# q of two mLSTM heads as plain blocks ahead of the seven-product doubles, and the blocks beside the attention moved on

## The chip, the cores and the metric

The kernel runs on one core of a Trainium2 chip. The time is device microseconds of one launch, as the median of several runs. Five engines work side by side, each through its own queue of instructions in order: TensorE (PE, matmuls, with its weight loads as PEld), VectorE (DVE), ScalarE (ACT), GpSimd (POOL) and SyncE (SP). Here SP issues the loads of weights and POOL most of the stores.

## The reference

Two layers over 1024 latent tokens and 256 context tokens of width 1024. Layer 0 runs 16 neighbourhood-attention heads beside 4 mLSTM heads of 256 columns; layer 1 is a gated recurrence (HGRN2). The change is in layer 0 alone, in how the input projection of the mLSTM heads is computed and when.

```python
def _ab_mixer(h_lat, h_ctx, w_in, b_gate, q_norm, k_norm, rpb, h_norm, w_out, need_ctx):
    def project(h, rotary):
        qa, ka, va, za, qb, kb, vb, ob, zb, g = _split_cols(h @ w_in, AB_SIZES)
...
        qb, kb = _heads(qb, ML_HEADS), _heads(kb, ML_HEADS) * (ML_DIM ** -0.5)
        if rotary:
            qb, kb = _axial_rope(qb), _axial_rope(kb)
...
    oa_l = _neighbourhood_attention(qa_l, ka_l, va_l, ka_c, va_c, rpb)
    hb_l, hb_c = _mlstm_bidir(mb_l, mb_c, need_ctx)
...
        ya = oa.reshape(oa.shape[:2] + (NA_WIDTH,)) * jax.nn.silu(za)
        yb = hb.reshape(hb.shape[:2] + (ML_WIDTH,)) * jax.nn.silu(zb)
        return jnp.concatenate([ya, yb], axis=-1) @ w_out
```

So each mLSTM head needs five blocks of 256 columns of `h @ w_in`: q and k (rotated for the latent tokens only), v, o and z. All is in fp32.

## The kernel before

**Precision.** Every fp32 operand is split into a high and a low part (`split`, L74 the high part on ACT, L75 the low part on DVE), and every product is three matmuls: high by high, high by low, low by high (`dense`, L127 to L129). The normed input lies transposed in memory as `hh` and `hl`, 1280 columns of tokens (ten row tiles of 128) by eight slices of 128 along the width.

**Plain blocks.** `proj_out` computes one block of 256 columns: for each pair of row tiles 2 x 8 x 3 matmuls into the psum buffer `mm`, one eviction into the buffer `ev` (there are two) with or without a gate (copy for v, tanh for o, tanh and a product for z), and one store by POOL to `md`, where the mLSTM reads it later. `ml_ahead(part, h)` is such a block of head h; `na_values(b)` ("n2") is the same for values of the attention.

**Doubles.** q and k of two heads together are 512 columns, and they are computed by Strassen's scheme in Winograd's form with seven products of half size instead of eight (`q_two` makes the first two products and `q_seven` the other five). The sums of quarters of the input that it needs are made on DVE and ACT by `q_sums`: "2" builds s2, s4 and s3 in memory of their own, "1" overwrites quarter 21 of `hh`/`hl` in place, which is restored by a DMA when all doubles are done. Each product's psum is added up on DVE (`sa`, `tr` and `mm` are the psum buffers, `qu` and `qv` the partial sums), the last addition writes `ev`, and for q and k the four instructions of `rope` (L999 to L1002) rotate `ev` in place ahead of the store.

**Stages of layer 0 on the chip,** in us of the span: norm and gates to about 220; the stage of `a_ahead` (sums, two plain blocks, four doubles: q and k of heads 0 and 1, q and k of heads 2 and 3) to 488; the attention in eight groups of two heads (`na_attn(p2, ...)`, ten tiles each) to 1372; the mLSTM (`ml_all`, steps g) to about 1765, with the output projection beside its second half.

**What sets the order.** A scheduler with a model of times orders the instructions of each stage; program order is the priority. The table `ahead` says which plain block is issued in which attention group, as work for PE beside the softmax; `issue_after(self.at[i])` holds a block back until tile i of the last group. `ML_AHEAD` does the same for the mLSTM: key -1 is its start, key g its step g, under `filler()`, which gives the block the lowest priority. The weights of the output projection are loaded into the buffers "w" that plain blocks use and into memory that `hh` leaves.

Of the kernel before, what the change touches and what calls it, by code (L numbers as in the profile page):

```python
# [9 lines left out]
F32 = mybir.dt.float32  # L10
# [8 lines left out]
P = 128  # L19
D = 1024  # L20
KD = D // P
LAT = 1024
# [3 lines left out]
EPS = 1e-6  # L26
NEG = -1.0e30

ML_AHEAD = {-1: ("o", 3), 2: ("z", 3)}
ML_ORDER = [8, 9, 4, 5, 6, 7, 0, 1, 2, 3]  # L30
ML_OUT = {1: (8, 8, 9, 9, 10, 10, 11, 11, 12, 12), 0: (13, 14, 14, 15, 16, 17, 18, 20, 22, 24)}

# [14 lines left out]
class Prog:  # L47
# [221 lines left out]
    def proj_out(self, c0, dst, gate=None, rev=False):  # L269
        nc = self.nc  # L270
        w = self.wring([self.a["wab"][:, c0 : c0 + 256]], 256)
        for tt in range(0, NT, 2)[:: -1 if rev else 1]:

            ps = self.ps("mm", [P, 2, 256])
            for j in range(2):
                self.proj_nat(ps[:, j, :], w, tt + j, 0, 256)
            v = self.t(self.wp, [P, 2, 256], F32, "ev", self.evb)
            if gate is None:
                nc.scalar.copy(v, ps)
            else:  # L280
                gate(v, ps)
            nc.gpsimd.dma_start(out=dst[tt * P : (tt + 2) * P, :].rearrange("(j p) f -> p j f", p=P), in_=v)


# [3 lines left out]
    def gate_z(self, out, ps):  # L288
        self.gate_o(out, ps)
        self.nc.vector.scalar_tensor_tensor(out=out, in0=out, scalar=1.0, in1=ps, op0=ALU.add, op1=ALU.mult)  # L290


    @contextmanager
# [6 lines left out]

    def ml_ahead(self, part, h, rev=False):
        c0 = (4 + "qkvoz".index(part)) * D + h * 256
        gate = {"o": self.gate_o, "z": self.gate_z}.get(part)
        dst = self.md[(part, h)] = self.md_all[len(self.md)]
        self.proj_out(c0, dst, gate, rev)

# [672 lines left out]
    def ml_sink(self, part, h, pool):  # L979
        dst = []  # L980
        for c in range(2):
            dst.append(self.md_all[len(self.md)])
            self.md[(part, h + c)] = dst[c]

        def sink(c, t, m, o):
            if part in "qk" and t < LAT // P:
                self.rope(o, t, m, pool)
            self.q_store(dst[c], t, m, o)

        return sink  # L990

    def rope(self, o, t, m, pool):
        tt = self.nc.vector.tensor_tensor
        s = self.t(self.qsr[0], [P, 512], F32, *self.qsr[1:])[:, 0 : m * 256]
        v4 = lambda x: x.rearrange("p (x b c) -> p x b c", b=2, c=64)
        tab = lambda i: (
            self.ropet[:, i, t : t + m].rearrange("p t a c -> p (t a) c").unsqueeze(2).to_broadcast([P, 2 * m, 2, 64])
        )
        tt(out=v4(s), in0=v4(o), in1=tab(1), op=ALU.mult)  # L999
        tt(out=v4(o), in0=v4(o), in1=tab(0), op=ALU.mult)  # L1000
        tt(out=v4(o)[:, :, 0, :], in0=v4(o)[:, :, 0, :], in1=v4(s)[:, :, 1, :], op=ALU.subtract)
        tt(out=v4(o)[:, :, 1, :], in0=v4(o)[:, :, 1, :], in1=v4(s)[:, :, 0, :], op=ALU.add)  # L1002

    def a_ahead(self, pool):
        nc, a = self.nc, self.a
        self.ropet = self.t(pool, [P, 2, 8, 2, 64], F32, "mrope", 1)
        nc.sync.dma_start(out=self.ropet, in_=a["rope"])
        a21 = self.q_quarter("21")
        for c in range(2):
            for i in range(self.half):  # L1010
                s = slice(i * P, (i + 1) * P)
                nc.gpsimd.dma_start(out=self.a21[c, :, :, s], in_=a21[c][:, :, s])
        S = {}
        self.q_sums(pool, "2", S)
        self.ml_ahead("v", 1, True)
        self.ml_ahead("o", 0, True)
        S["1"] = a21
        self.q_sums(pool, "1", S)
        todo = [(p, h) for h in (0, 2) for p in "qk"]
        cols = [[(4 + "qkvoz".index(p)) * D + (h + c) * 256 for c in range(2)] for p, h in todo]  # L1020
        sinks = [self.ml_sink(p, h, pool) for p, h in todo]
        us = [self.q_two(self.q_raw(pool, cols[i], ("11", "21")), S, sinks[i], pool) for i in range(2)] + [None] * 2
        for i in range(len(todo)):
            self.q_seven(self.q_raw(pool, cols[i]), S, sinks[i], pool, us[i])
        for c in range(2):
            nc.gpsimd.dma_start(out=a21[c], in_=self.a21[c])
# [191 lines left out]
    def build(self):  # L1218
        self.six = None
        tc, nc, a = self.tc, self.nc, self.a  # L1220
        dma = nc.sync.dma_start
        with ExitStack() as es:
# [21 lines left out]
            def load(name, shape, eng=nc.gpsimd):  # L1244
# [13 lines left out]
                out=self.qkn, in0=qkn[:, 0:1], scalar1=qkn[:, 1:2], scalar2=0.125, op0=ALU.mult, op1=ALU.mult  # L1258
# [57 lines left out]
            with tc.tile_pool(name="na", bufs=2) as pool, tc.tile_pool(name="wx", bufs=2) as wx, self.pp.phase(tq=1, s=2, acc=1):  # L1316
                self.six = [(self.wp, "w", 4)] * 4 + [(wx, "w", 2)] * 2
                qk = self.na_qk(0, pool)
                z = self.na_z(0, pool)
                self.ml_ahead("z", 0)  # L1320
                ahead = {1: ["n2"], 2: ["n3"], 3: ["o1"], 4: ["z1"], 5: ["v2"], 6: ["o2"], 7: ["z2", "v3"]}
                for p2 in range(8):
                    self.na_attn(p2, qk, z, pool)
                    if p2 < 7:
                        qk = self.na_qk(p2 + 1, pool)
                    for i, x in enumerate(ahead.get(p2, [])):
                        with tc.issue_after(self.at[(3, 6)[i]]) if p2 == 7 else nullcontext():
                            self.na_values(int(x[1])) if x[0] == "n" else self.ml_ahead(x[0], int(x[1]))
                    if p2 < 7:
                        z = self.na_z(p2 + 1, pool)  # L1330
# [268 lines left out]
```

## Time and profile before

| what | value |
|---|---|
| timed runs | 3545.17, 3551.78, 3552.8 us, median 3551.78 |
| profiled execution | 3541.76 us, its span 3539.9 us |
| instructions | 64788, of them 24378 matmuls |
| PE, PEld busy | 98%, 89% |
| DVE, ACT, POOL busy | 68%, 45%, 15% |
| mean DMA rate | 102 GB/s |

A window's row gives, for a stretch of the span, each engine's busy time and in brackets its instructions, then the clock granted to PE as a share of full speed, the busy share of the DMA engines and what they moved. A row of the waits says which engine and line waited for which, for how long in total, how often, and the longest. A row of the timeline is one instruction or a run of like ones, with the idle time ahead of it in square brackets. A row of a tile's view gives the count and the shortest, median and longest duration in ns, with the first and last start. All matmuls are pipelined, so the time one takes from the next is read from the count in a full window, not from its duration.

### The profile page before, as it was taken

To read this page: it belongs to the slowest core of one execution; us is meant where nothing else is said; L and a number is where in the kernel's file an instruction comes from. 1 tells how busy PE (TensorE), PEld (TensorE's weight loads), DVE (VectorE), ACT (ScalarE), POOL (GpSimd) and SP (SyncE) were. 2 spreads that over 40 slices of the span, in tenths; PEclk is the share of its full clock that TensorE was granted. 3 is DMA by queue.
4 is the path that set the end of the run, shared out by engine and by line. 5 is a ranking of instruction groups with operands and counts; after the bars stand their busy time and mean duration, and the time that the engine had idled before them with its cause. 6 is when DMAs were issued, how large, how long until landed. Compare 5 with 4: busy or idle time off the path is not lost.

```text
span 3539.9 us, 64788 instructions
## 1 busy us (share of the span) xinstructions
PE 3460.8 (98%) x24378; PEld 3144.3 (89%) x24378; DVE 2390.2 (68%) x6044; ACT 1597.8 (45%) x3691; POOL 524.6 (15%) x838
## 2 busy tenths in 40 slices
PE   8998999999999999999999999999999999999989
PEld 5898999999999989887778999989999999999877
DVE  4668866766666654666767766577777777777853
ACT  5532225555455534555547333344444444444431
POOL 3210121222222211111211111000000100000010
PEclk9999999999999999999999999999999999999999
DMA  7542332222223224544474222212111211211354
GB/s 234 179 155 78 93 115 72 74 77 79 83 80 86 72 83 154 162 139 147 125 250 147 102 100 101 87 31 60 61 48 52 63 49 49 60 60 49 108 176 125
DMA packets 372649, 359.71 MB, mean 102 GB/s; under 512 B 30072, under 2 KB 322872, under 8 KB 372208
## 3 DMA queue, kind: packets, MB, share of 16 engines
q1 hardware_dynamic: 328944, 248.25, 23.8%
q0 software_dynamic: 43392, 107.32, 9.0%
q8 instruction: 193, 3.16, 0.4%
q14 instruction: 120, 0.98, 0.1%
HBM read 274.00 MB, written 81.32 MB: 100 GB/s over the span
## 4 chain that ended last, share of the span: by engine, by line
PE 81%; issue 9%; DMA 3%; DVE 2%; ACT 2%; POOL 1%; SPq 0%; POOLq 0%; ACTq 0%; DVEq 0%
PE mm L129 14%; PE mm L127 14%; PE mm L128 14%; PE s L1126 6%; PE acc L689 2%; PE tr L669 2%; PE sa L128 2%; PE sa L127 2%; PE sa L129 2%; PE acc L472 2%; PE s L479 1%; PE s L1171 1%; PE mm L743 1%; PE mm L744 1%; PE mm L745 1%
## 5 line engine op out<-in xcount | busy, mean ns | idle before, releaser
L127 PE MATMUL mm<-wh,hh 128*128 128x256 f32 x2120 | 608.1, 287 | 2.4 <-ACT ev L545 1.5
L128 PE MATMUL mm<-wl,hh 128*128 128x256 f32 x2120 | 608.4, 287 | 0.7 <-DVE wl L75 0.7
L129 PE MATMUL mm<-wh,hl 128*128 128x256 f32 x2120 | 608.4, 287 | 0.4 <-DVE hl L75 0.4
L129 PE MATMUL mm<-hh,wl 128*128 128x512 f32 (+1 forms) x1344 | 490.9, 365 | 0.0
L127 PE MATMUL mm<-hh,wh 128*128 128x512 f32 (+1 forms) x1344 | 485.0, 361 | 0.0
L128 PE MATMUL mm<-hl,wh 128*128 128x512 f32 (+1 forms) x1344 | 483.9, 360 | 0.0
L127 PEld LDWEIGHTS mm<-wh,hh 128*128 128x128 f32 x2120 | 404.6, 191 | 9.9 <-issue 3.7
L128 PEld LDWEIGHTS mm<-wl,hh 128*128 128x128 f32 x2120 | 404.8, 191 | 5.1 <-DVE wl L75 0.9
L129 PEld LDWEIGHTS mm<-wh,hl 128*128 128x128 f32 x2120 | 404.4, 191 | 5.3 <-issue 1.5
L74 ACT CAST wh<-wraw 128x512 fp32r<-128x512 f32 x282 | 173.5, 620 | 261.2 <-PE mm L128 127.2
L128 PEld LDWEIGHTS mm<-hl,wh 128*128 128x128 f32 x1344 | 254.0, 189 | 32.2
L129 PEld LDWEIGHTS mm<-hh,wl 128*128 128x128 f32 x1344 | 253.9, 189 | 30.2
L127 PEld LDWEIGHTS mm<-hh,wh 128*128 128x128 f32 x1344 | 254.3, 189 | 29.2
L1117 ACT COPY gksel<-gK 128x512 f32<-128x512 f32 x224 | 147.0, 663 | 214.3 <-PE s L1126 205.2
L75 DVE TENSOR_TENSOR wl<-wraw,wh 128x512 fp32r<-128x512 f32 x282 | 190.6, 686 | 60.0 <-ACT wh L74 58.3
L1126 PE MATMUL s<-gQ,gksel 128*128 128x128 f32 x1536 | 199.8, 276 | 0.0
L1126 PEld LDWEIGHTS s<-gQ,gksel 128*128 128x128 f32 x1536 | 192.4, 191 | 7.0
L743 PE MATMUL mm<-woh,yh 128*128 128x512 f32 x444 | 180.2, 407 | 6.1 <-ACT woh L74 3.3
L745 PE MATMUL mm<-woh,yl 128*128 128x512 f32 x444 | 177.9, 401 | 1.0 <-DVE yl L75 0.9
L744 PE MATMUL mm<-wol,yh 128*128 128x512 f32 x444 | 177.7, 400 | 0.0
L74 ACT CAST wh<-b 128x512 fp32r<-128x512 f32 x130 | 80.8, 622 | 199.5 <-PE sa L129 100.3
L1147 DVE TENSOR_TENSOR gQ<-gQ,gT 128x256 f32<-128x256 f32 x384 | 143.3, 414 | 28.1 <-PE s L1126 28.1
(457 smaller groups left out, 8646.9 us busy)
## 6 DMA issues: line engine op xcount, KB each, us to landing
wraw<-yd SPq DMA_DIRECT2D x144, 256.0 KB
wraw<-in_wc_dram SPq DMA_DIRECT2D x128, 256.0 KB
wraw<-in_wab_dram SPq DMA_DIRECT2D x92, 256.0 KB
md<-ev POOLq DMA_DIRECT2D x92, 256.0 KB, 2.8
adar<-in_wada_dram POOLq DMA_DIRECT2D x32, 512.0 KB, 4.8
b<-in_wc_dram SPq DMA_DIRECT2D x64, 256.0 KB
vzd<-qo POOLq DMA_DIRECT2D x56, 256.0 KB, 2.5
adar<-in_wada_dram SPq DMA_DIRECT2D x16, 512.0 KB
```

What stands on the lines that cost most here:

```text
L74: nc.scalar.copy(hi, x)
L75: nc.vector.tensor_tensor(out=lo, in0=x, in1=hi.bitcast(F32), op=ALU.subtract)
L127: mm(ps, lhsT=lh(k), rhs=rh(k), start=(first and k == 0), stop=False)
L128: mm(ps, lhsT=lh(k), rhs=rl(k), start=False, stop=False)
L129: mm(ps, lhsT=ll(k), rhs=rh(k), start=False, stop=(last and k == nk - 1))
L472: nc.tensor.matmul(num, lhsT=qc[:, j, :], rhs=C[d][:, j, :], start=False, stop=(j == 1))
L743: mm(ps, lhsT=yh[:, k, :], rhs=w.h(kk), start=(kk == 0), stop=False)
L744: mm(ps, lhsT=yh[:, k, :], rhs=w.l(kk), start=False, stop=False)
L745: mm(ps, lhsT=yl[:, k, :], rhs=w.h(kk), start=False, stop=(kk == 8 * len(qs) - 1))
L1117: nc.scalar.copy(ksel.rearrange("p (b s i) -> p b s i", s=2, i=h), pick(K))
L1126: nc.tensor.matmul(pa[:, c, :].rearrange("p (b s i) -> p b s i", s=2, i=h), lhsT=ksel[:, c * P : (c + 1) * P], rhs=qp[:, c * nbc : (c + 1) ...
L1147: nc.vector.tensor_tensor(out=t[:, i, :, s, :], in0=t[:, i, :, s, :], in1=bc(tot), op=ALU.mult)
```

## The change

In `a_ahead` one of the four doubles goes (q of heads 2 and 3); those two q are computed as plain blocks with a new gate, `gate_q`, which copies on ACT and rotates in place on DVE, with the scratch buffer `qv2` in place of `qs`. They stand between v of head 1 and the sums "1", where o of head 0 stood. o of head 0 becomes the first block beside the attention; the blocks that follow move on by one place, and v of head 3 moves into the start of the mLSTM, whose o and z follow at steps 1 and 4 instead of the start and step 2. In the last attention group the two blocks are held back to tiles 0 and 5 instead of 3 and 6. `rope` takes the scratch buffer as an argument.

```diff
-ML_AHEAD = {-1: ("o", 3), 2: ("z", 3)}
+ML_AHEAD = {-1: ("v", 3), 1: ("o", 3), 4: ("z", 3)}
...
-                gate(v, ps)
+                gate(v, ps, *[tt] * (gate == self.gate_q))
...
+    def gate_q(self, out, ps, tt):
+        self.nc.scalar.copy(out, ps)
+        if tt < LAT // P:
+            self.rope(out.rearrange("p a b -> p (a b)"), tt, 2, self.qrt)
...
-        gate = {"o": self.gate_o, "z": self.gate_z}.get(part)
+        gate = {"o": self.gate_o, "z": self.gate_z, "q": self.gate_q}.get(part)
...
-    def rope(self, o, t, m, pool):
+    def rope(self, o, t, m, home):
         tt = self.nc.vector.tensor_tensor
-        s = self.t(self.qsr[0], [P, 512], F32, *self.qsr[1:])[:, 0 : m * 256]
+        s = self.t(home[0], [P, 512], F32, *home[1:])[:, 0 : m * 256]
...
+        self.qrt = (pool, "qv2", 2)
...
         self.q_sums(pool, "2", S)
         self.ml_ahead("v", 1, True)
-        self.ml_ahead("o", 0, True)
+        self.ml_ahead("q", 2, True)
+        self.ml_ahead("q", 3, True)
         S["1"] = a21
         self.q_sums(pool, "1", S)
-        todo = [(p, h) for h in (0, 2) for p in "qk"]
+        todo = [("q", 0), ("k", 0), ("k", 2)]
...
-        us = [self.q_two(self.q_raw(pool, cols[i], ("11", "21")), S, sinks[i], pool) for i in range(2)] + [None] * 2
+        us = [self.q_two(self.q_raw(pool, cols[i], ("11", "21")), S, sinks[i], pool) for i in range(2)] + [None]
...
-                self.ml_ahead("z", 0)
-                ahead = {1: ["n2"], 2: ["n3"], 3: ["o1"], 4: ["z1"], 5: ["v2"], 6: ["o2"], 7: ["z2", "v3"]}
+                self.ml_ahead("o", 0)
+                ahead = {1: ["z0"], 2: ["n2"], 3: ["n3"], 4: ["o1"], 5: ["z1"], 6: ["o2"], 7: ["z2", "v2"]}
...
-                        with tc.issue_after(self.at[(3, 6)[i]]) if p2 == 7 else nullcontext():
+                        with tc.issue_after(self.at[(0, 5)[i]]) if p2 == 7 else nullcontext():
```

How the order moves, at three places. First DVE among the quarter sums ahead of the products, in the order before (`qs` are the sums, L75 the low parts of a split):

```order
L75 TENSOR_TENSOR s2l_2109<-qs_2127,s2h_2108 128x4x128
L860 TENSOR_TENSOR qs_2127<-qs_2127,hh_126 128x512
L860 TENSOR_TENSOR qs_2127<-qs_2127,hl_127 128x512
L75 TENSOR_TENSOR s4l_2115<-qs_2127,s4h_2114 128x4x128
L838 TENSOR_TENSOR qs_2141<-hl_127 128x512
L839 TENSOR_TENSOR qs_2140<-qs_2140,qs_2141 128x512
```

The same place on DVE after, where L1005 to L1008 are a rotation at the eviction of a plain q (lines 6 further down than before):

```order
L75 TENSOR_TENSOR s2l_2109<-qs_2127,s2h_2108 128x4x128
L866 TENSOR_TENSOR qs_2127<-qs_2127,hh_126 128x512
L866 TENSOR_TENSOR qs_2127<-qs_2127,hl_127 128x512
L1005 TENSOR_TENSOR qv_450_2618<-ev_2616,mrope_2089 128x512
L75 TENSOR_TENSOR s4l_2115<-qs_2127,s4h_2114 128x4x128
L1006 TENSOR_TENSOR ev_2616<-ev_2616,mrope_2089 128x512
L844 TENSOR_TENSOR qs_2141<-hl_127 128x512
L1007 TENSOR_TENSOR ev_2616<-ev_2616,qv_450_2618 128x4x64
L1008 TENSOR_TENSOR ev_2616<-ev_2616,qv_450_2618 128x4x64
L845 TENSOR_TENSOR qs_2140<-qs_2140,qs_2141 128x512
```

The four instructions of a rotation now stand between the sums, one or two sums apart. Second, PE in the first tiles of the last attention group, in the order before (`s` are scores, `tr` transposes, `acc` the product with the values):

```order
L632 MATMUL s_16171<-akh_15372,aqs_15370 128x264
L633 MATMUL s_16171<-akl_15374,aqs_15370 128x264
L619 MATMUL s_16211<-akh_15371,aqs_15369 128x256
L620 MATMUL s_16211<-akl_15373,aqs_15369 128x256
L669 MATMUL tr_16186<-ident_73,aP_16164 96x128 x2
L669 MATMUL tr_16186<-ident_73,aP_16164 72x128
```

The first tile of that group on PE after (`mm` with `hh` and `hl` is a plain block):

```order
L625 MATMUL s_15837<-akh_15070,aqs_15068 128x256
L626 MATMUL s_15837<-akl_15072,aqs_15068 128x256
L638 MATMUL s_15842<-akh_15070,aqs_15068 128x264
L639 MATMUL s_15842<-akl_15072,aqs_15068 128x264
L127 MATMUL mm_16532<-wh_16509,hh_126 128x256
L128 MATMUL mm_16532<-wl_16508,hh_126 128x256
L129 MATMUL mm_16532<-wh_16509,hl_127 128x256
```

Block matmuls now stand in this group from its first tile. Third, PE at the end of the last plain block beside the mLSTM, in the order before (`tr`, `s` and `acc` with names that begin with m are the mLSTM's own):

```order
L128 MATMUL mm_18253<-wl_18035,hh_126 128x256
L129 MATMUL mm_18253<-wh_18036,hl_127 128x256
L526 MATMUL tr_18880<-ident_73,mhs_3241_18641 128x128
L407 MATMUL s_18892<-mqT_3296_18788,mkT_18795 128x128 x2
L526 MATMUL tr_18835<-ident_73,mhs_3252_18666 128x128
L479 MATMUL s_18913<-mvw_18911,mkn_3120_18335 128x258
```

The same end on PE after:

```order
L128 MATMUL mm_18489<-wl_18271,hh_126 128x256
L129 MATMUL mm_18489<-wh_18272,hl_127 128x256
L406 MATMUL tr_19476<-ident_73,mkn_3512_19474 128x128 x2
L485 MATMUL s_19545<-mvw_19541,mkn_3419_19196 128x258
L400 MATMUL tr_19487<-ident_73,mqn_19485 128x128 x2
L406 MATMUL tr_19494<-ident_73,mkn_3519_19492 128x128 x2
```

Before, 37 rows lie between that end and the first matmul of the output projection, in step 8 of the mLSTM; after, 15 rows, in step 10.

More of the change, by code (lines that the diff above doesn't have):

```diff
@@ L986, in sink @@
             if part in "qk" and t < LAT // P:
-                self.rope(o, t, m, pool)
+                self.rope(o, t, m, self.qsr)
             self.q_store(dst[c], t, m, o)
         return sink
-    def rope(self, o, t, m, pool):
+    def rope(self, o, t, m, home):
         tt = self.nc.vector.tensor_tensor
-        s = self.t(self.qsr[0], [P, 512], F32, *self.qsr[1:])[:, 0 : m * 256]
+        s = self.t(home[0], [P, 512], F32, *home[1:])[:, 0 : m * 256]
         v4 = lambda x: x.rearrange("p (x b c) -> p x b c", b=2, c=64)
```

## The prediction

> **What bounds the kernel now.** The page comes first: one engine is full, and the chain that ended last runs on it.
>
> ```profile
> span 3539.9 us, 64788 instructions
> PE 3460.8 (98%) x24378; PEld 3144.3 (89%) x24378; DVE 2390.2 (68%) x6044; ACT 1597.8 (45%) x3691; POOL 524.6 (15%) x838
> PE 81%; issue 9%; DMA 3%; DVE 2%; ACT 2%; POOL 1%; SPq 0%; POOLq 0%; ACTq 0%; DVEq 0%
> ```
>
> TensorE is 98% busy and carries 81% of the chain. A matmul more costs its time unless it falls into a hole, and a hole closed is a gain. So I read the windows next, stage by stage, looking for holes near the places that the change touches.
>
> ```profile
> core 0: us, PE busy (x) PEld busy (x) DVE busy (x) ACT busy (x) POOL busy (x), PEclk, DMA share, GB/s
> 280.00:360.00 80.00, 67.60 (x510) 64.04 (x509) 68.84 (x131) 14.27 (x24) 8.77 (x14) 0.96 0.27 79
> 360.00:440.00 80.00, 80.00 (x674) 80.00 (x674) 67.70 (x139) 16.56 (x28) 14.56 (x22) 1.00 0.30 95
> 1270.00:1290.00 20.00, 15.38 (x120) 12.19 (x119) 13.72 (x56) 9.31 (x31) 3.28 (x5) 0.91 0.44 126
> 1300.00:1320.00 20.00, 20.00 (x185) 19.39 (x184) 10.57 (x38) 7.00 (x22) 4.68 (x7) 1.00 0.29 86
> 1478.00:1504.00 26.00, 20.01 (x92) 15.79 (x92) 21.33 (x64) 18.86 (x52) 5.37 (x12) 0.87 0.90 275
> ```
>
> Row two is the price list. It lies wholly in the products: 674 matmuls of 256 columns in 80 us, 0.1187 us each, TensorE full, VectorE at 67.70/80 = 85%. The other rows show three holes.
>
> *Hole 1, where the products begin (280 to 360):* 510 matmuls where the same product work has 674, so 164 are missing: 164 x 0.1187 = **19.5 us** (idle 12.4 plus 0.04 x 80 of clock gives 15.6; some records may be absent). The waits from 285 to 356, the timeline and a window of 10 us name the cause.
>
> ```profile
> DVE ev L932 <- DMA md<-ev: 7.0, 4, 2.9
> PE sa L127 <- DVE qu L956: 3.5, 1, 3.5
> 331.70 0.58 PE L127 MATMUL sa<-wh,s4h 128*128 128x256 f32 x1 [3.50 <-DVE qu L956]
> 330.00:340.00 10.00, 8.30 (x48) 8.30 (x49) 9.05 (x21) 1.24 (x2) 2.00 (x3) 0.66 0.19 66
> ```
>
> TensorE waits for an accumulator that VectorE has not added up: VectorE, 68.84 of 80 busy, carries the quarter sums, the weight splits and the first rotations at once. The 3.50 us wait is followed by a granted clock of 0.66 over 10 us, so it costs 3.4 us more.
>
> The Trainium skill, "TensorE: Matmul & The Clock Gate", section on the HAM clock gate, says that half clock follows an idle window of about 3.4 us; by that rule only waits of that length cost clock, and this one agrees.
>
> *Hole 2, the last attention group (1270 to 1290):* idle 4.62 and 0.09 x 20 = 1.8 of clock, **6.4 us**. The same windows for tile mm alone:
>
> ```profile
> core 0: us, PE busy (x), PEclk, DMA share, GB/s
> 1270.00:1290.00 20.00, 2.01 (x18) 0.91 0.44 126
> 1300.00:1320.00 20.00, 14.17 (x107) 1.00 0.29 86
> ```
>
> With 107 projection matmuls among the attention TensorE is full; with 18 it is not. The filler is missing there.
>
> *Hole 3, the recurrence of the mLSTM (1478 to 1504):* idle 5.99 and 0.13 x 26 = 3.4 of clock, **9.4 us**. Rows of the timeline, and one of the waits:
>
> ```profile
> 1478.30 0.28 PE L129 MATMUL mm<-wh,hl 128*128 128x256 f32 x1
> ...
> 1487.15 0.33 PE L526 MATMUL tr<-ident,mhs 128*128 128x128 f32 x1 [2.44 <-ACT myt L527]
> 1489.71 0.69 PE L394 MATMUL tr<-ident,mqn 128*128 128x128 f32 x2 [2.23 <-ACT myt L527]
> ...
> 1503.57 0.58 PE L743 MATMUL mm<-wh,yh 128*128 128x512 f32 x1
> ACT woh L74 <- DMA wraw<-in_woab_dram: 3.7, 2, 2.8
> ```
>
> It opens at the last matmul of the last plain block and closes at the first of the output projection. Between them ScalarE stands in its queue behind a cast that waits 3.7 us for the output weights, and the copies that TensorE needs stand behind it.
>
> **The change part by part.** Sums go against the profiled execution, 3541.76 us (its span and 1.86 around it). The median of the runs is 3551.78, 10.0 above it; I take the difference from the profile and add it to the median.
>
> *1. A double less, two plain blocks more.* A double by seven products is 7 x 60 = 420 matmuls, a plain block 10 row tiles x 8 x 3 = 240. Two blocks replace one double: 480 - 420 = 60 more, x 0.1187 = **+7.1 us**. All of it counts, since TensorE is full on both sides. The double's additions on VectorE go too, at nothing: in 360:440 VectorE leaves 12 us of 80 free beside a full TensorE. Weights loaded are the same 2 MB. Stores on GpSimd fall from 12 (48 of L963 in four doubles, rows below) to 10 at 730 ns, off the path.
>
> *2. q of two heads ahead of the products.* In the order of TensorE 480 matmuls of q now precede the sums that the products need, where 240 of o stood: 240 x 0.1187 = 28.5 us more of work that asks little of VectorE. What it asks:
>
> ```profile
> L282 POOL DMA_DIRECT2D md<-ev x60: 712/730/808, 155.6 to 1481.2; - x60
> L963 POOL DMA_DIRECT2D md<-ev x48: 570/707/735, 309.3 to 490.8; - x48
> L279 ACT COPY ev<-mm x40: 568/587/604, 57.0 to 1370.2; 128x512 f32<-128x512 f32 x40
> L999 DVE TENSOR_TENSOR qs<-ev,mrope x40: 411/681/692, 305.5 to 488.3; 128x512 f32<-128x512 f32 x24, 128x256 f32<-128x256 f32 x16
> L1000 DVE TENSOR_TENSOR ev<-ev,mrope x40: 414/680/693, 307.6 to 489.1; 128x512 f32<-128x512 f32 x24, 128x256 f32<-128x256 f32 x16
> L1001 DVE TENSOR_TENSOR ev<-ev,qs x40: 280/415/426, 308.5 to 489.8; 128x256 f32<-128x256 f32 x24, 128x128 f32<-128x128 f32 x16
> L1002 DVE TENSOR_TENSOR ev<-ev,qs x40: 281/414/420, 308.7 to 490.1; 128x256 f32<-128x256 f32 x24, 128x128 f32<-128x128 f32 x16
> L75 DVE TENSOR_TENSOR wl<-wraw,wh 128x512 fp32r<-128x512 f32 x282 | 190.6, 686 | 60.0 <-ACT wh L74 58.3 <-PE tr L1101 0.9
> ```
>
> A rotation is 0.681 + 0.680 + 0.415 + 0.414 = 2.19 us. Each block has four (its two context tiles are not rotated): 8 x 2.19 = 17.5. Four more weight splits of 0.686 make 2.7. VectorE gets 20.2 us of work in 28.5 us of TensorE, so it comes to the products with less arrears. At full pace the arrears shrink by 28.5 - 20.2 = 8.3, at its 85% by 28.5 - 23.8 = 4.7; the middle is 6.5. When the arrears fall by that, the 3.50 us wait may fall under what costs clock, worth another 3.4 us: at even chance 1.7. Together **-8.2 us**. Below it is bounded by nothing repaid (0), if VectorE's queue only moves its waits; above by the whole hole, 19.5. I take 8.2 since VectorE's own row, not another resource, names the wait. Next late after it: the stores of the two eviction buffers (7.0 us in the waits).
>
> The ScalarE copies (0.587 each, ten for q against five tanh of o before) lie beside TensorE: in 280:360 ScalarE is busy 14.27 of 80. If that cover were gone, five copies are 2.9 us.
>
> *3. Blocks beside the attention.* o0 moves from ahead of the attention to its first place, every other one step later, v3 out of it: nine blocks before and after, so no matmul more or less. What changes is the last group: its two blocks may now issue at tiles 0 and 5, not 3 and 6, and in the new order block matmuls stand in every tile of it. Hole 2 closes: **-6.4 us**; bounds 0 (the weights come late) and -6.4. The price is one of place: the 57 us of filler lie over ten tiles instead of seven, still 5.7 per tile where 1300:1320 holds 107 x 0.1187 = 12.7 in 20 us.
>
> *4. Three blocks beside the mLSTM instead of two.* The third (240 x 0.1187 = 28.5 us, already counted in 1) fills what hole 3 leaves open: the last block ends two steps later, and 15 instead of 37 rows of TensorE separate it from the output projection. But the output weights still need the buffers of the last block and must be loaded behind it, at a DMA share of 0.90 in this window. Bounds: -9.4 if the hole goes, +3.7 if ScalarE meets one more such wait for weights. Nearer to the middle, and a little to the side of no change for the DMA's sake: **-2 us**.
>
> Of that window the Trainium skill's rule on the 3.4 us idle window would make less: its longest waits are 2.44 and 2.23 us, and yet the clock fell to 0.87. By the rule the hole would be worth 6.0, by the row 9.4; the row decides.
>
> Sum: 7.1 - 8.2 - 6.4 - 2.0 = **-9.5 us**: 3532.3 profiled, 3542.3 as a median.
>
> **The rivals.**
>
> *B, the whole hole 1 goes.* VectorE's arrears turn out under what the accumulators buffer, so no wait is left: 7.1 - 19.5 - 6.4 - 2.0 = -20.8, **3531.0**. For it: TensorE is already full from 360 on with VectorE at 85%, so arrears do not grow in steady state. Against it: 8.3 at most is gained against 19.5.
>
> *C, slower: VectorE stands behind the rotations.* Its queue is in order, and in the new order the four instructions of a rotation stand among the sums of quarter 21, which the products wait for. A rotation needs its two row tiles finished by TensorE (48 x 0.1187 = 5.7 us). The buffer it holds passes copy 0.59, rotation 2.19, issue 0.73 and landing:
>
> ```profile
> md<-ev POOLq DMA_DIRECT2D x92, 256.0 KB, 2.8
> ```
>
> That is 6.3 us of the 11.4 in which one of two buffers must come free. It decides once a rotation waits over 5.1 us in VectorE's queue, the length of seven or eight sums. If each of eight then holds TensorE for 1.5 us, +12, and VectorE, which stood still itself, repays nothing of hole 1: 7.1 + 12 - 6.4 - 2.0 = +10.7, **3562.5**. For it: stores already delay evictions by 7.0 us; against it: four to six of the sums stand between a rotation's parts, not eight.
>
> *D, the holes only move.* Sums of quarter 21 are still a burst, only later, and VectorE meets it as late as now; hole 3 follows the last block. Only hole 2 closes: 7.1 - 6.4 = +0.7, **3552.5**. For it: the work of the sums itself is unchanged, and they cannot be taken ahead of the blocks that read quarter 21.
>
> *E, only TensorE's work counts.* The fillers that close hole 2 are missing elsewhere among the attention, nothing is returned: +7.1, **3558.9**. Against it: the windows of hole 2 show the hole without filler and, 30 us later, none with it. The Trainium skill, "Perfetto Trace Analysis", section Identifying the Most-Contended Engine, says to improve first the engine with the highest occupancy; by that alone a change that gives TensorE more work loses.
>
> **How the numbers follow.** A measurement of this kernel tells no change from 0.2%, which is 7.1 us. Forecast 0.51; B 0.17; D 0.15; C 0.12; E 0.05. The forecast's own range, with part 2 from -4.7 to -11.7 and part 4 from +3.7 to -9.4 not both at an end, is -16 to -3 (3536 to 3549): 0.36 of its 0.51 lies beyond -7.1. Faster 0.36 + 0.17 = 0.53; same 0.15 + 0.13 of D + 0.03 of C and E = 0.31; slower 0.02 of D + 0.03 of E + 0.11 of C = 0.16. The range holds the forecast, D, E and the upper half of B and leaves out C and B with hole 3 gone: 3529 to 3559.
>
> **What would show it.** In the new profile: 60 matmuls more; no wait of over 3 us for qu in the first two doubles (part 2), one of that length or a clock under 0.9 there speaks for D; stretches of mm under 5 us of 20 absent from the last attention group (part 3); a shorter stretch between the last plain block and the first output matmul (part 4). Evictions of q that hold TensorE at mm, or sums of quarter 21 late behind a rotation, would be C. The forecast is wrong if holes 1 and 3 together return under 4 or over 18 us.

## The result, and the profile after

The changed kernel takes 3530.03 us (median of four runs, 3526.28 to 3532.8) against 3550.51 of the kernel before on the same chip: 0.9944 of it, 95% interval 0.9927 to 0.9961. A second comparison later gave 0.9948 (0.9936 to 0.9960), 3528.37 against 3547.40. So the change is worth 18 to 20 us. The forecast was 9.5 us faster, 3542.3: the direction is right and the gain was undersized by half. The wide range (3529 to 3559) holds the time by one microsecond; the forecast's own range (3536 to 3549) does not.

The page of the changed kernel: its span, the busy time of the engines, and the chain that ended last:

```profile
span 3529.6 us, 64866 instructions
PE 3462.1 (98%) x24438; PEld 3151.1 (89%) x24438; DVE 2370.4 (67%) x6001; ACT 1598.3 (45%) x3692; POOL 521.4 (15%) x836
PE 83%; issue 8%; DMA 3%; DVE 2%; ACT 2%; POOL 1%; SPq 0%; POOLq 0%; DVEq 0%; ACTq 0%
```

60 matmuls more (24438 against 24378), as worked out. Where their cost came back is read from whole stages. The bounds of the windows are the same four instructions in every kernel: the first product's matmul, the first transpose of the attention, its last product with the values, the last output transpose of the mLSTM. Products, attention and mLSTM before:

```profile
256.70:495.50 238.80, 224.93 (x1829) 221.12 (x1827) 197.59 (x385) 51.74 (x88) 36.79 (x53) 0.99 0.33 101
495.50:1356.30 860.80, 855.95 (x7328) 809.57 (x7326) 558.59 (x1763) 432.89 (x1166) 184.30 (x239) 1.00 0.28 79
1356.30:1791.30 435.00, 416.67 (x2293) 356.94 (x2288) 268.72 (x830) 240.24 (x663) 84.16 (x225) 0.99 0.50 153
```

The same three after:

```profile
287.30:466.30 179.00, 172.19 (x1415) 171.33 (x1414) 147.80 (x288) 39.52 (x68) 30.37 (x43) 0.98 0.37 113
466.30:1334.60 868.30, 866.55 (x7450) 822.76 (x7448) 557.15 (x1763) 434.34 (x1170) 184.27 (x240) 1.00 0.28 78
1334.60:1773.10 438.50, 428.50 (x2403) 370.71 (x2399) 271.64 (x832) 243.03 (x667) 83.85 (x227) 0.99 0.50 155
```

First column minus second is TensorE's idle time: 13.9, 4.9 and 18.3 us before, 6.8, 1.8 and 10.0 after. All three holes shrink. The attention can be read in a second way: its stage is 7.5 us longer and holds 122 matmuls more, which are 14.5 us at 0.1187, so it gives 7.0 us back.

Hole 1 is not gone. Windows over its remains, and the waits in them:

```profile
350.00:370.00 20.00, 17.54 (x135) 17.36 (x134) 15.33 (x32) 2.48 (x4) 3.43 (x5) 0.91 0.36 113
440.00:460.00 20.00, 15.87 (x118) 15.49 (x118) 15.44 (x32) 3.50 (x6) 4.73 (x7) 0.91 0.38 119
363.48 0.36 PE L127 MATMUL mm<-wh,s2h 128*128 128x256 f32 x1 [2.46 <-DVE ev L938]
452.24 0.36 PE L127 MATMUL mm<-wh,hh 128*128 128x256 f32 x1 [2.67 <-DVE ev L938]
```

Full windows of 20 us hold 168 such matmuls; these hold 135 and 118. The 83 missing are 9.9 us, where before 164 were missing (19.5 us). TensorE still waits for VectorE's last additions. The second stretch is at a new place: it lies near the end of the products, which end at 466.3, while the kernel before was full there. Its last double, in two windows:

```profile
460.00:470.00 10.00, 10.00 (x86) 10.00 (x85) 7.31 (x16) 2.44 (x4) 2.00 (x3) 1.00 0.32 101
470.00:480.00 10.00, 10.00 (x87) 10.00 (x86) 7.69 (x16) 1.28 (x3) 2.01 (x3) 1.00 0.49 132
```

So a part of the loss is later rather than gone. The run without rotation (below) has this stretch full too, so VectorE's arrears reach that far. Holes 2 and 3 after, the second as windows of the last tiles and of tile mm alone, the third by the last block's end and the first output matmul:

```profile
1270.00:1290.00 20.00, 18.25 (x165) 16.98 (x164) 12.90 (x43) 9.55 (x26) 4.14 (x6) 1.00 0.46 135
1270.00:1290.00 20.00, 11.60 (x86) 1.00 0.46 135
1497.03 0.28 PE L129 MATMUL mm<-wh,hl 128*128 128x256 f32 x1
...
1503.51 0.41 PE L400 MATMUL tr<-ident,mqn 128*128 128x128 f32 x2 [2.02 <-DMA mqn<-md]
1508.52 0.58 PE L749 MATMUL mm<-wh,yh 128*128 128x512 f32 x1
```

86 block matmuls stand among these tiles instead of 18. The stretch without blocks beside the mLSTM is 11.5 us long instead of 25.

At the end of the mLSTM the change is 18.2 us ahead (1773.1 against 1791.3), but its span is only 10.3 shorter. 4.4 us are lost at the very end, after the last store is issued. Its rows in the timelines, before and after:

```profile
3536.21 0.54 POOL L1458 DMA_DIRECT2D out_dram<-oxh  x1 [10.23 <-DVE oxh L783]
```

```profile
3521.48 0.54 POOL L1466 DMA_DIRECT2D out_dram<-oxh  x1 [10.23 <-DVE oxh L789]
```

To the ends of the spans (3539.9 and 3529.6) it is 3.7 us before and 8.1 after. The other 3.5 us went in the stages behind the mLSTM, which vary by as much between executions of one kernel.

### The profile page after: what moved, and what is told of

Read it like the earlier page. It is cut to its first block, busy times and chain, and to the rows that moved or that the text cites. A ratio compares the mean times of both kernels' runs of the same rounds, so it can differ in the third digit from the quotient of the medians.

```text
span 3529.6 us, 64866 instructions
## 1 busy us (share of the span) xinstructions
PE 3462.1 (98%) x24438; PEld 3151.1 (89%) x24438; DVE 2370.4 (67%) x6001; ACT 1598.3 (45%) x3692; POOL 521.4 (15%) x836
## 4 chain that ended last, share of the span: by engine, by line
PE 83%; issue 8%; DMA 3%; DVE 2%; ACT 2%; POOL 1%; SPq 0%; POOLq 0%; DVEq 0%; ACTq 0%
PE mm L129 15%; PE mm L128 15%; PE mm L127 15%; PE s L1134 6%; PE acc L695 3%; PE tr L675 2%; PE sa L128 2%; PE sa L127 2%; PE sa L129 2%; PE acc L478 2%; PE s L485 2%; PE s L1179 1%; PE mm L749 1%; PE mm L750 1%; PE mm L751 1%
## 5 line engine op out<-in xcount | busy, mean ns | idle before, releaser
L127 PE MATMUL mm<-wh,hh 128*128 128x256 f32 x2256 | 648.8, 288 | 3.8 <-DVE ev L938 2.7
L128 PE MATMUL mm<-wl,hh 128*128 128x256 f32 x2256 | 648.8, 288 | 2.0 <-DVE wl L75 1.9
L129 PE MATMUL mm<-wh,hl 128*128 128x256 f32 x2256 | 648.4, 288 | 0.0
L127 PEld LDWEIGHTS mm<-wh,hh 128*128 128x128 f32 x2256 | 431.1, 191 | 11.8 <-issue 6.9
L128 PEld LDWEIGHTS mm<-wl,hh 128*128 128x128 f32 x2256 | 431.4, 191 | 7.3 <-DVE wl L75 2.8
L129 PEld LDWEIGHTS mm<-wh,hl 128*128 128x128 f32 x2256 | 431.0, 191 | 3.6 <-issue 0.7
L75 DVE TENSOR_TENSOR wl<-wraw,wh 128x512 fp32r<-128x512 f32 x282 | 191.2, 686 | 53.8 <-ACT wh L74 51.2
```

What stands on the lines that cost most here:

```text
L75: nc.vector.tensor_tensor(out=lo, in0=x, in1=hi.bitcast(F32), op=ALU.subtract)
L127: mm(ps, lhsT=lh(k), rhs=rh(k), start=(first and k == 0), stop=False)
L128: mm(ps, lhsT=lh(k), rhs=rl(k), start=False, stop=False)
L129: mm(ps, lhsT=ll(k), rhs=rh(k), start=False, stop=(last and k == nk - 1))
```

## The experiments

All times are medians; each kernel was compared with the kernel before on the same chip. "Tail opened" means that the two blocks of the last attention group are held back to tiles 0 and 5 instead of 3 and 6. Idle is TensorE's in products, attention and mLSTM, from the windows described; what a lower clock costs is not in it. The end of the program is 4.4 us longer in some kernels than in others (last section); that is in the times.

| kernel | time, before beside it | ratio (95%) | idle, us |
|---|---|---|---|
| before (first profile) | | | 13.9 / 4.9 / 18.3 |
| before again | 3548.7, 3547.8 | 1.0001 (0.9993 to 1.0010) | 16.8 / 5.1 / 18.2 |
| before, tail opened | 3537.4, 3547.8 | 0.9967 (0.9955 to 0.9979) | 15.0 / 1.5 / 16.9 |
| change, tail undone | 3536.3, 3547.8 | 0.9962 (0.9949 to 0.9974) | 6.4 / 4.6 / 12.4 |
| q and o ahead only | 3528.5, 3547.8 | 0.9946 (0.9934 to 0.9958) | 0.3 / 5.2 / 17.0 |
| moves only | 3552.8, 3545.3 | 1.0022 (1.0013 to 1.0030) | 31.7 / 2.0 / 12.3 |
| change, two beside mLSTM | 3524.2, 3545.3 | 0.9943 (0.9930 to 0.9955) | 0.3 / 1.8 / 16.0 |
| change, no rotation | 3518.0, 3545.3 | 0.9924 (0.9911 to 0.9937) | 0.0 / 2.0 / 10.0 |
| q and o ahead, tail opened | 3524.1, 3545.3 | 0.9940 (0.9928 to 0.9953) | 0.0 / 1.5 / 17.0 |
| change again | 3528.4, 3547.4 | 0.9948 (0.9936 to 0.9960) | 6.8 / 1.9 / 10.1 |
| q and o ahead, tail opened, again | 3522.9, 3547.4 | 0.9936 (0.9924 to 0.9947) | 0.3 / 1.5 / 15.8 |
| change, half rotation on GpSimd | 3527.9, 3547.4 | 0.9946 (0.9934 to 0.9957) | 2.4 / 1.9 / 10.9 |
| eight blocks beside attention | 3535.9, 3547.4 | 0.9967 (0.9956 to 0.9979) | 0.0 / 6.5 / 15.4 |

**Before again** (no edit).

> The kernel before, unchanged, with a second profile. Its profiled execution took 3541.76 us, its timed runs 3545 to 3553 (median 3550.5), while the changed kernel's profiled execution (3531.36) lies among its timed runs (3526 to 3533). Between the two profiles 10.4 us are found, between the medians 20.5. Theory one, the three holes as in the forecast: the profiled pair is the typical one, a second profile shows the same losses of TensorE in each stage within 2 us, and the other 10 us are a wait that comes and goes from execution to execution. Rival, the first profile was a lucky one: a second profile takes about 3550 and shows 8 to 10 us more of lost time in one of the three places that the change touches, most likely where the products begin, where 20 us are lost in the first profile.

The second profile took 3552.24 us, 10.5 more than the first. The stage of gates and norm, which the change does not touch, carries most of it. The first row is the first profile, the second this one:

```profile
0.00:220.00 220.00, 207.43 (x1322) 159.36 (x1323) 117.03 (x223) 111.14 (x200) 58.10 (x94) 0.98 0.62 199
0.00:220.00 220.00, 203.90 (x1267) 153.33 (x1268) 115.38 (x220) 110.33 (x199) 57.35 (x93) 0.98 0.62 197
285.00:365.00 80.00, 65.33 (x494) 61.19 (x492) 66.96 (x127) 15.78 (x26) 8.60 (x13) 0.98 0.24 75
```

55 matmuls fewer fit into the first 220 us, and the first product starts at 264.7 instead of 256.7. So 8 of the 10.5 us come and go ahead of the change's place. In other kernels this start varies too: the change's two profiles start their products at 287.3, the same kernel with the tail undone at 292.6. The products are 2.6 us longer (241.4 against 238.8), most of it in hole 1: 494 of 674 matmuls, 21.4 us instead of 19.5. The attention's 2.8 us more and the 3.1 less behind the mLSTM cancel. Theory one holds in the main, since most of the difference is a stage that comes and goes; the rival had the time right (about 3550) but not the place. What makes the first stage vary was not followed further.

**The tail alone, and undone.** The first edit on the kernel before, the second on the change:

```diff
-  with tc.issue_after(self.at[(3, 6)[i]]) if p2 == 7 else nullcontext():
+  with tc.issue_after(self.at[(0, 5)[i]]) if p2 == 7 else nullcontext():
```

```diff
-  with tc.issue_after(self.at[(0, 5)[i]]) if p2 == 7 else nullcontext():
+  with tc.issue_after(self.at[(3, 6)[i]]) if p2 == 7 else nullcontext():
```

> The kernel before with one number pair changed: the two blocks of the last attention group are held back to tiles 0 and 5 instead of 3 and 6. Forecast's theory: hole 2 closes, 6.4 us faster than before, the products and the mLSTM unchanged. Rival (the whole gain is hole 1): no change, 0 to -1. If the filler were only missing later, the loss would show among tiles 6 to 9 instead: 0.

> The changed kernel with the two blocks of the last attention group held back to tiles 3 and 6 again. Forecast's theory: hole 2 opens again, 6 us slower than the changed kernel, so 14 us faster than before. Rival (the whole gain is hole 1): as fast as the changed kernel, 20 us faster than before.

Alone it gives 10.4 us (interval 7.5 to 16), undone it takes 6 to 8 of the change's gain. The attention's idle time goes from 4.9 to 1.5 and from 1.8 back to 4.6. The tiles that were short are full:

```profile
1270.00:1290.00 20.00, 20.00 (x182) 18.93 (x180) 10.35 (x35) 6.67 (x19) 1.33 (x2) 1.00 0.37 114
500.20:1369.10 868.90, 867.38 (x7454) 823.28 (x7454) 560.42 (x1765) 436.07 (x1171) 186.62 (x242) 1.00 0.28 79
```

The second row, against before's, has 8.1 us and 126 matmuls more: 126 x 0.1187 - 8.1 = 6.9 us. The rival that all is hole 1 is out. The stage's 6.9 us lie a little below the interval of the times (7.5 to 16); where the rest of the 10.4 comes from is not shown.

**q and o ahead, nothing else** (the change's products; lists, hold-back and mLSTM of before).

```diff
         self.ml_ahead("v", 1, True)
+        self.ml_ahead("o", 0, True)
         self.ml_ahead("q", 2, True)
         self.ml_ahead("q", 3, True)
...
-                self.ml_ahead("o", 0)
+                self.ml_ahead("z", 0)
```

> Three doubles and q of the last two heads as plain blocks ahead, but o of head 0 left ahead of the products too, and the blocks beside attention and mLSTM, and the hold-back, as before. So only the first two parts of the change, with 57 us instead of 28.5 us of plain work more ahead of the products. Forecast's theory: +7.1 for 60 matmuls, hole 1 shrinks from 20 us to under 10 (more slack than in the change, so rather 4 to 8), holes 2 and 3 as before: 5 to 10 us faster than before. Rival B (hole 1 is all): 12 to 14 us faster. Rival D (the hole only moves): 5 to 7 us slower than before.

19 us faster, more than any theory here said: hole 1 is gone to 0.3 us idle and full clock, over the whole stage.

```profile
317.50:485.50 168.00, 167.73 (x1408) 167.39 (x1407) 135.06 (x267) 36.18 (x63) 28.97 (x42) 1.00 0.39 118
```

VectorE is busy 135 of 168 us: with 114 us of plain work ahead it arrives in time. This is rival B's mechanism, which the change itself does not reach with 85.5 us ahead. The forecast's theory put 4 to 8 us left in the hole and is too high by that. The stage is 70.8 us shorter than before's with 421 matmuls fewer (50.0 us), so the hole returns 20.8 us, or 23.5 against the second profile of before; less the 7.1 us of 60 matmuls that makes 13.7 to 16.4. The interval of the 19 us measured reaches down to 15.

**The moves alone** (four doubles; only v of head 1 ahead; lists, hold-back and mLSTM of the change).

```diff
         self.ml_ahead("v", 1, True)
-        self.ml_ahead("o", 0, True)
...
-                self.ml_ahead("z", 0)
+                self.ml_ahead("o", 0)
```

> The last two parts of the change without the first two: four doubles as before, but only v of head 1 ahead of the products, o of head 0 first beside the attention, the other blocks moved on and held back as in the change. No matmul more than before. Theory of the slack (each 28.5 us of plain work ahead of the products takes 10 to 12 us off the hole where they begin: 25 us lost with 57 us ahead, 12 with 85.5, 2 with 114): that hole grows from 25 to about 36, the attention group and the mLSTM give 7 each back, 1 to 4 us faster than before. Rival (the hole is fixed by the double's own work, the order of the blocks does not matter): the hole stays at 25, 13 to 15 us faster than before.

7.5 us slower than before, 4.4 of them at the end of the program, which is long here and short before (last section). Windows and waits, with the slow start of the products in the first row:

```profile
230.00:290.00 60.00, 39.83 (x296) 37.99 (x295) 52.52 (x83) 17.93 (x33) 0.73 (x1) 0.80 0.20 59
230.80:492.30 261.50, 229.80 (x1828) 225.05 (x1827) 219.44 (x416) 56.18 (x96) 37.08 (x54) 0.93 0.31 94
PE sa L127 <- ACT s2h L74: 14.8, 2, 7.6
```

The products idle 31.7 us, and the clock of 0.93 over 261.5 us costs 18 more. The direction of the slack theory holds and the rival (order does not matter) is out; its size, linear at 10 to 12 us a block, is too small here. With 28.5 us ahead the wait is no longer for an accumulator but for the sums themselves (s2h, 14.8 us in two waits), and the granted clock is 0.50 from 270 to 297, from the first of these waits until well past the second.

**Two blocks beside the mLSTM** (on the change; v of head 3 early, beside the gates).

```diff
-ML_AHEAD = {-1: ("v", 3), 1: ("o", 3), 4: ("z", 3)}
+ML_AHEAD = {-1: ("o", 3), 2: ("z", 3)}
...
                 self.ml_ahead("v", 0)
+                self.ml_ahead("v", 3)
```

> The changed kernel with part four undone: v of head 3 is taken far ahead, beside the gates, and beside the mLSTM stand two blocks at the start and step 2 as before. The number of matmuls is the change's. Theory (the third block fills the hole of the mLSTM): 6 to 7 us of loss come back there, 11 to 13 us faster than before instead of 18 to 20. Forecast's size of that part: 2 us. Rival (the hole follows whatever block is last, a smaller loss is chance): as fast as the change within 1.5 us. The products get no more slack, since the added block stands before the quarter sums begin.

The mLSTM's idle time rises from 10.0 to 16.0 as the theory said, so the third block does fill hole 3. But the kernel is as fast as the change (0.9943), for the other half of the expectation fell: the block beside the gates gives the products slack all the same, and their idle time drops from 6.8 to 0.3.

```profile
316.10:484.00 167.90, 167.61 (x1409) 167.41 (x1408) 135.25 (x267) 36.21 (x63) 29.06 (x42) 1.00 0.39 118
1354.40:1774.50 420.10, 404.08 (x2164) 343.35 (x2159) 266.20 (x828) 238.47 (x658) 81.97 (x222) 0.98 0.51 156
```

**No rotation** (q of heads 2 and 3 left unrotated).

```diff
         self.nc.scalar.copy(out, ps)
-        if tt < LAT // P:
-            self.rope(out.rearrange("p a b -> p (a b)"), tt, 2, self.qrt)
```

> The changed kernel without the rotation at the eviction of the two plain q; these q stay unrotated. 8 x 2.19 = 17.5 us of VectorE's work ahead of the products are gone, the matmuls stay. Theory of VectorE's arrears: the 12 us still lost in the products fall to 0 to 4, so 26 to 30 us faster than before. Rival one, the two eviction buffers and their stores set what is left: 12 us stay lost, 18 to 20 us faster than before. Rival C of the forecast (VectorE stands behind rotations in the plain blocks) would show as lost time of TensorE before the products, which the profile of the change does not have: 0.

```profile
293.90:461.30 167.40, 167.40 (x1407) 167.27 (x1407) 139.44 (x273) 37.45 (x65) 29.05 (x43) 1.00 0.38 117
```

Idle 0.0, 27 us faster than before. The eviction buffers and their stores are the same as in the change, so they do not set what is left of hole 1; VectorE's 17.5 us of rotations do. (Without a rotation a buffer is also held for less time, but in the change's plain blocks TensorE does not pay for that: its idle time from 220 to the first product is 0.2 us.) By the same 0.2 us, rival C's wait in the plain blocks is absent from the change's profile.

**Half of the rotation on GpSimd.**

```diff
-        tt(out=v4(s), in0=v4(o), in1=tab(1), op=ALU.mult)
-        tt(out=v4(o), in0=v4(o), in1=tab(0), op=ALU.mult)
+        mul(out=v4(s), in0=v4(o), in1=tab(1), op=ALU.mult)
+        mul(out=v4(o), in0=v4(o), in1=tab(0), op=ALU.mult)
...
-            self.rope(out.rearrange("p a b -> p (a b)"), tt, 2, self.qrt)
+            self.rope(out.rearrange("p a b -> p (a b)"), tt, 2, self.qrt, self.nc.gpsimd.tensor_tensor)
```

> The changed kernel with the two multiplications of each rotation of the plain q on GpSimd instead of VectorE; the two additions stay on VectorE. VectorE has 8 x 1.36 = 10.9 us less ahead of the products. Theory of the arrears: the 12 us lost in the products fall to 2 to 4, so 8 to 10 us faster than the change, 26 to 30 faster than before, the best so far. Rival: a multiplication on GpSimd, which no trace here shows, takes several us, the two eviction buffers are held longer and VectorE waits in its queue for it: lost time of TensorE in the plain blocks, no faster than the change or slower.

No faster: 3527.9 against 3528.4 of the change beside it. The two windows are the plain blocks and the products:

```profile
220.00:295.00 75.00, 70.58 (x566) 70.03 (x565) 63.66 (x83) 19.61 (x34) 30.24 (x24) 0.95 0.32 101
295.00:465.00 170.00, 167.59 (x1409) 167.39 (x1408) 146.61 (x285) 39.45 (x68) 33.15 (x46) 1.00 0.39 117
L1006 POOL TENSOR_TENSOR qv<-ev,mrope x8: 1288/1342/2919, 242.7 to 298.3; 128x512 f32<-128x512 f32 x8
L1007 POOL TENSOR_TENSOR ev<-ev,mrope x8: 1611/1624/1636, 244.1 to 299.7; 128x512 f32<-128x512 f32 x8
ACT s2h L74 <- DVE qs L866: 15.1, 3, 6.1
PE mm L127 <- ACT wh L74: 2.0, 1, 2.0
```

The products lose 2.4 us instead of 6.8 idle and 3.6 of clock. The plain blocks, full in the change, now lose 4.4 idle and 0.05 x 75 = 3.8 of clock: ScalarE stands behind casts of the sums (s2h, 15.1 us), and the weights of the next plain block are cast behind them in its queue (2.0 of the 4.4 us; in the other 2.4 TensorE waits for the low part of weights, from VectorE).

The sums are late because the 10.9 us of VectorE's work that the theory took off did not come off. VectorE's rows from 240 to 300, two of the change and two of this run, and two instructions side by side:

```profile
240.00:270.00 30.00, 30.00 (x252) 30.00 (x251) 26.64 (x47) 8.64 (x15) 3.63 (x5) 1.00 0.29 89
270.00:300.00 30.00, 30.00 (x252) 30.00 (x251) 27.17 (x49) 10.32 (x18) 2.90 (x4) 1.00 0.30 89
240.00:270.00 30.00, 25.58 (x193) 25.18 (x192) 27.84 (x33) 7.32 (x13) 15.73 (x12) 0.89 0.20 63
270.00:300.00 30.00, 27.59 (x230) 27.39 (x230) 25.72 (x35) 8.63 (x15) 14.90 (x13) 1.00 0.19 58
248.89 1.94 DVE L844 TENSOR_TENSOR qs<-hl 128x512 f32<-128x512 f32 x1
248.97 1.31 POOL L1006 TENSOR_TENSOR qv<-ev,mrope 128x512 f32<-128x512 f32 x1
```

VectorE is busy 53.6 us with 68 instructions, where the change has 53.8 us with 96. The instruction of L844, 0.69 us in the change, takes 1.94 us while GpSimd multiplies, and others beside a multiplication take 1.2 to 2.4 us. So neither text has the cause: GpSimd's multiplication takes 1.3 and 1.6 us, not several, and VectorE waits for one only once (1.2 us), but its own instructions get longer beside it.

**q and o ahead with the tail opened.** The edit of "q and o ahead" with tiles 0 and 5. It ran twice, the second time beside the change.

> Both gains that did not depend on each other: q of two heads ahead with o of head 0 kept there too, and the blocks of the last attention group held back to tiles 0 and 5; the blocks otherwise as before, two beside the mLSTM. Theory of separate holes: 19 us (the first) and 6 to 10 (the second) add up, 25 to 29 us faster than before, about 3521, and faster than the change. Rival (filler taken early in the last group is missing later, or in the mLSTM): no faster than the first alone, 19.

> q of two heads and o of head 0 ahead, hold-back at tiles 0 and 5, two blocks beside the mLSTM, a second time, now beside the change itself. By the stages of its first profile it loses 11 us less in the products than the change and 5.5 more in the mLSTM: 3 to 6 us faster than the change. Rival: equal to the change within 1 us, since the 60 plain matmuls and the same 15 blocks fill holes of one size wherever they stand.

21 and 25 us faster than before by the medians (expected 25 to 29); the second time 3522.9 against 3528.4 of the change, 5.5 us or 0.16% less. Their intervals against before (0.9924 to 0.9947 and 0.9936 to 0.9960) still touch, but five of its six runs are faster than all five of the change, so that it beats the change is very likely. The gains of the two parts add up in the idle times (0.3 and 1.5), and the mLSTM's 15.8 is the price. And 4.4 of the 5.5 us may be the end alone: this kernel has the short one, the change the long one (last section).

**Eight blocks beside the attention** (the kernel above, with v of head 3 moved from the last attention group into the mLSTM).

```diff
-ML_AHEAD = {-1: ("o", 3), 2: ("z", 3)}
+ML_AHEAD = {-1: ("v", 3), 1: ("o", 3), 4: ("z", 3)}
...
-  ahead = {..., 7: ["z2", "v3"]}
+  ahead = {..., 7: ["z2"]}
```

> q of two heads and o of head 0 ahead, three blocks beside the mLSTM, and so only eight beside the attention (one in the last group, from tile 0). All three other holes are filled; theory of a fixed stock of filler (fifteen blocks in all, one too few for every hole): the block taken from the attention leaves 5 to 28 us of lost time there, most in the last group, and the mLSTM gains 6, so slower than the kernel with nine blocks beside the attention by 0 to 20 us. Rival (the attention has filler to spare): 5 to 7 us faster than that kernel, 27 us faster than before.

13 us slower than the same kernel with nine. The attention's end shows the hole again:

```profile
1300.00:1330.00 30.00, 24.06 (x176) 19.30 (x174) 17.66 (x69) 11.98 (x39) 3.38 (x5) 0.81 0.27 72
1513.47 0.69 PE L406 MATMUL tr<-ident,mkn 128*128 128x128 f32 x2 [4.33 <-ACT mkT L408]
```

5.9 us idle and 0.19 x 30 = 5.7 of clock. The mLSTM gained nothing either (15.4): three blocks are in it, yet after them it stands 4.33 us for one copy of ScalarE. So three blocks there are not enough by themselves; why it waits longer here than in the change stays open.

## Why the prediction was right, and where it was off

- **Part 1, +7.1:** 60 matmuls more, as counted. No run isolates its time; the sum below uses it.
- **Part 2, -8.2:** the mechanism is shown (no rotation: 0.0 idle; moves only: 31.7; o kept ahead: 0.3). No run takes a double away with the same work ahead, so what that alone gives the hole is not separated. The idle time of the products fell by 7.1 (13.9 to 6.8), inside the 4.7 to 8.3 worked out from VectorE's work; by missing matmuls it is 19.5 to 9.9, -9.6, and -11.5 from the second profile of before (21.4). The 1.7 us carried for the clock did not come back: the 3.50 us wait is gone, but the two new waits of 2.46 and 2.67 us each cost 0.09 x 20 = 1.8 us of clock, together as much as it had.
- **Part 3, -6.4:** -7.0 by the count of matmuls, a little beyond its bound of -6.4; -6.9 with the tail alone opened.
- **Part 4, -2.0:** this is the term that was mis-sized. Idle 18.3 to 10.0 is -8.3, near its bound of -9.4. The argument that the output weights would wait behind the last block in the same way put the value too near to nothing. That wait did come (ScalarE stands 3.3 us for them, 3.7 before), but TensorE's two long waits in the stretch without blocks are 1.14 and 2.02 us, not 2.44 and 2.23, and the stretch fell from 25 to 11.5 us. With two blocks the idle time came back to 16.0; but three blocks were not enough by themselves in the run with eight beside the attention (15.4), so what makes the difference is only in part shown.
- **The sum** to the end of the mLSTM: 7.1 - 9.6 to 11.5 - 7.0 - 8.3 = -17.8 to -19.7; the first pair of profiles shows -18.2 there. By the lengths of the stages against their matmuls more or fewer it is -10.7 in the products, -7.0 in the attention, -9.6 in the mLSTM, +2.1 ahead of the products (where 28.5 us of block took 30.6) and +7.1 for the 60 matmuls: -18.1. The 4.4 us at the end were in no term. Between the medians lie 18 to 20 all the same, mostly because the profile taken as the base had an early first stage (8 us before its second) and lay 10 us under its median. The account closes to about 4 us, the size of what the first stage and the stages behind the mLSTM vary by; it does not close further.
- **The forecast's own sign** of being wrong was that holes 1 and 3 together return under 4 or over 18 us. They return 17.9 in the first pair (9.6 by missing matmuls and 8.3 by idle time), 19.8 against the second profile of before, and 20.3 by the lengths of the stages. So it lies at this limit or beyond it: the mechanisms held, the two sizes did not. That the time still lies in the stated range is owed to its reaching down to rival B, by one microsecond, and is luck.
- **Rivals.** B came nearest to the time (3531.0), by luck, since not in its way: hole 1 kept half. D and E are out: all three holes shrank, though more than half of what is left of hole 1 stands at a later place. C did not occur in the change. With GpSimd's help the sums did come late for the plain blocks, but because VectorE's instructions got longer, not because they stood behind a rotation. The slack that B asks for exists, one block further.

## What to carry to other kernels

A block of independent matmuls is a stock of filler with a fixed size. Paying for more of it (here 7 us) is worth it when it lets another engine finish its preparation first, and its price is read from the hole, not from the arithmetic saved. Count the holes and the blocks before distributing them: fifteen blocks closed all the holes at once in none of the placements tried here, and each block taken from one place came back as idle time there. Where one profile lies off the median, find the stage that varies before taking it as the base.

## What the runs showed of the hardware

A wait shorter than the 3.50 us of the forecast's example can cost clock too. Around the 2.46 us wait of the change, and after a wait of 1.80 us before (rows of the windows in this order: the change from 360, from 364, before from 351):

```profile
360.00:364.00 4.00, 1.54 (x13) 1.36 (x12) 3.33 (x7) 0.31 (x1) 1.15 (x3) 1.00 0.40 116
364.00:371.00 7.00, 7.00 (x49) 7.00 (x48) 3.58 (x9) 0.62 (x2) 0.36 (x1) 0.76 0.30 105
351.00:358.00 7.00, 5.88 (x49) 5.88 (x50) 6.36 (x14) 1.25 (x2) 0.57 (x1) 1.00 0.08 28
```

After 2.46 us the mean clock is 0.76 over 7 us, which is 3.4 us at half speed; after 1.80 us it stays at 1.00. But the length of a wait alone does not decide it. In the second profile of before a wait of 3.51 us left the clock at 1.00, and with the tail undone one of 1.97 us was followed by 0.83 over 10 us (a row of the window and the wait, of each):

```profile
334.00:347.00 13.00, 8.98 (x72) 8.40 (x71) 11.79 (x24) 1.24 (x2) 2.71 (x4) 1.00 0.28 93
339.65 0.39 PE L127 MATMUL sa<-wh,s4h 128*128 128x256 f32 x1 [3.51 <-DVE qu L956]
366.00:376.00 10.00, 8.03 (x55) 7.85 (x54) 6.62 (x16) 0.81 (x2) 1.82 (x3) 0.83 0.33 107
368.27 0.36 PE L127 MATMUL mm<-wh,s2h 128*128 128x256 f32 x1 [1.97 <-DVE ev L938]
```

What else decides was not tested, so the clock that a wait costs is read from the row behind it, not from its length. The Trainium skill, "TensorE: Matmul & The Clock Gate", section on the HAM clock gate, gives an idle window of about 3.4 us as the condition; the change's trace does not agree, since its wait of 2.46 us was a microsecond shorter and the clock still halved. And a multiplication of 128 x 512 in fp32 took 1.34 and 1.62 us (medians) on GpSimd, where VectorE takes 0.68; beside such a multiplication a VectorE instruction of 0.69 us took up to 2.4 us.

The end of the program comes in two lengths, and the three programs with two profiles have the same one in both. From the last store's issue to the end it is 8.1 us in the change (both profiles), with its tail undone, without rotation, with half the rotation on GpSimd, and with the moves alone; it is 3.7 us in the other kernels, before (both profiles) among them. The code there is the same. No single edit separates the two groups (eight blocks beside the attention has three beside the mLSTM and the short end), but a count does: every program with the long end issues twelve plain blocks behind the products (nine beside the attention, three beside the mLSTM), every one with the short end eleven. How that reaches the end of the program stays open; it is worth 4.4 us of the change's time.
